# A kurtosis kernel: the batch finish as a bracket summed on TensorE, and the last group squared in one stretch

## The chip, the cores and the metric

One core of one Trainium2 chip runs the kernel; the program uses no other. Its engines work side by side: TensorE (matrix products, into a memory called PSUM), VectorE and ScalarE (element by element), and SyncE, which starts the transfers (DMA, loads and stores). The metric is device time in microseconds (us) of the whole program, as the median of several runs. A run is fast or slow by the rule that a slow one is over 1.5% above the fastest of the same kernel; only fast runs enter a ratio. The profiler records every execution; the trace shown for a kernel is one of them.

## The reference

For each of 1024 rows of 8192 values: subtract the mean, divide by the standard deviation, take the mean of the fourth power, subtract 3.

```python
mean = np.mean(x, axis=-1, keepdims=True)
std = np.std(x, axis=-1, keepdims=True)
z = (x - mean) / (std + 1e-8)
return (np.mean(z ** 4, axis=-1) - 3).astype(np.float32)
```

With the centred sums s2 = Σ(x-mean)² and s4 = Σ(x-mean)⁴ over n values this is n·s4/s2² - 3.

## The kernel before

The rows come in 18 groups, numbered 0 to 17. Most hold 64 rows, each row spread over k = 2 partitions of 4096 columns: 2 MB per group. For groups 6 to 16, TensorE transposes the 32 blocks of 128 columns into one PSUM tile and so adds them up (`tps`); VectorE adds the partitions of a row (`red`); a matmul with a column of -1/n gives the negated mean (`mps`); ScalarE copies it (`nmu`) and squares the tile in place with it as bias, with the sum in `s2`. The fourth powers, squares of the squares, are split: ScalarE takes the first columns, VectorE the rest. In groups 0 to 5 VectorE adds up the columns instead; in group 17 both engines share that, and the large square is cut into two halves.

The parts that matter here (comments added):

```python
    for i in range(L):
        warm_up(WARM.get(i, 0))
        mean(i)                                # PE: tps x32, mps; DVE: red; ACT: nmu
        square(i)                              # ACT, the large square
        if i >= 1:
            fourth_dve(i - 1, GROUPS[i - 1][2])
            load_next(i - 1)                   # a buffer is free: next load
        for f in steps.get(i, ()):             # one step of a batch's finish
            next(f, None)
        fourth_act(i, 0, GROUPS[i][2])
```

Results are finished in four batches of groups. The first three are finished in three steps spread over later groups, 7-8-9, 9-10-11 and 13-14-15:

```python
    def finish(b):
        fac = factor(b)             # PE: p2 = row sums of s2, times -1/n; DVE: fac = -1/p2^2
        yield
        w4 = scaled(b, fac, len(b)) # DVE: (qa + qd) * fac
        yield
        result(b, [w4])             # PE: pk = w4 summed per row; DVE: kr = pk - 3; store
```

In the traces each engine runs its instructions in the order in which these calls issue them.

## Time and profile before

| | before |
|---|---|
| median of 4 runs | 97.75 us (97.65 to 97.93) |
| span of the execution whose trace is shown | 97.1 us (a run of 98.84 us) |
| busy: ScalarE, VectorE, TensorE | 82%, 79%, 63% |
| start of the last large square S(17), of the last product kr | 87.87, 94.88 us |

S(i) is the start of group i's large square; for group 17 before, that of its first half. The span is shorter than the time: in the other runs of this kernel the time is 1.7 us above the span. Note that the traced execution was 1.1 us slower than the median.

### The profile page before, as it was taken

What the parts mean: (1) busy time and instruction counts of PE and PEld (TensorE: products, weight loads), DVE (VectorE), ACT (ScalarE), POOL (GpSimd) and SP (SyncE); (2) the same over time, 40 slices, a digit from 0 to 9 for tenths busy, and PEclk for the clock granted to TensorE, in tenths of its full rate; (3) what the DMA queues carried; (4) which work ended last, traced back from release to release, by engine and by line L of the source; (5) the groups of instructions that cost most, each with busy time, mean ns of one, the idle gap of its engine ahead of it and who ended that gap; (6) DMA issues with size and microseconds to landing.
All of it is one profiled execution on the core that took longest, in us unless ns stands there. A gap on an engine that the chain in (4) does not pass through costs nothing.

```text
span 97.1 us, 1280 instructions
## 1 busy us (share of the span) xinstructions
PE 60.7 (63%) x446; PEld 53.3 (55%) x446; DVE 76.5 (79%) x86; ACT 79.6 (82%) x89; POOL 4.7 (5%) x19
## 2 busy tenths in 40 slices
PE   0040201119998979729979797978979697951330
PEld 0040201015287869629969697877969596941310
DVE  1336819899995936989089899898999998999980
ACT  6055360899999999999549999999999999999960
POOL 6830000000000000000000000000000000000000
PEclk9999999999999999996699999999999999997555
DMA  2989999999999999999999999999999999300000
GB/s 57 390 302 405 425 432 432 432 432 426 404 422 406 435 423 429 412 428 409 433 421 428 412 417 403 410 424 404 419 418 413 414 411 397 123 1 0 0 0 4
DMA packets 5226, 33.63 MB, mean 346 GB/s; under 512 B 612, under 2 KB 612, under 8 KB 3812
## 3 DMA queue, kind: packets, MB, share of 16 engines
q1 hardware_dynamic: 5220, 33.56, 84.1%
q8 instruction: 3, 0.05, 0.2%
q14 instruction: 3, 0.02, 0.1%
HBM read 33.55 MB, written 0.00 MB: 346 GB/s over the span
## 4 chain that ended last, share of the span: by engine, by line
ACT 34%; DMA 28%; DVE 17%; PE 12%; issue 7%; ACTq 0%; DVEq 0%; SPq 0%
ACT xt L176 29%; DMA xt<-in_x_dram 28%; DVE xt L188 10%; PE tps L132 9%; DVE junk L149 6%; ACT xt L183 4%; PE pk L226 1%; DVE red L138 1%; ACT nmu L170 1%; PE mps L168 1%; PE mps L159 1%; PE p L204 0%; ACT wa L290 0%; DVE qd L188 0%; DVE kr L228 0%
## 5 line engine op out<-in xcount | busy, mean ns | idle before, releaser
L188 DVE CUSTOM_DVE_ANT_0 xt<-xt 128x3456 f32<-128x3456 f32 (+7 forms) x19 | 58.9, 3103 | 3.2 <-ACT xt L176 1.8
L176 ACT ACTIVATE xt<-xt,nmu 128x4096 f32<-128x4096 f32 (+2 forms) x19 | 60.4, 3177 | 0.6
L132 PE MATMUL tps<-ident,xt 128*128 128x128 f32 x380 | 45.8, 280 | 1.4 <-DMA xt<-in_x_dram 1.4
L132 PEld LDWEIGHTS tps<-ident,xt 128*128 128x128 f32 x380 | 43.6, 146 | 2.0 <-issue 1.4
L149 DVE CUSTOM_DVE_ANT_0 junk<-xt 128x2048 bf16<-128x2048 f32 (+3 forms) x7 | 10.2, 1453 | 6.9 <-DMA xt<-in_x_dram 6.9
L159 PE MATMUL mps<-part,blk 128*128 128x1 f32 x12 | 3.2, 332 | 19.3 <-DVE part L149 19.3
L159 PEld LDWEIGHTS mps<-part,blk 128*128 128x128 f32 x12 | 3.0, 304 | 20.7 <-issue 9.6
L183 ACT ACTIVATE xt<-xt 128x640 f32<-128x640 f32 (+5 forms) x15 | 12.9, 859 | 0.5
L170 ACT COPY nmu<-mps 128x1 f32<-128x1 f32 x18 | 2.6, 147 | 12.5 <-PE mps L159 10.0
L138 DVE TENSOR_REDUCE red<-tps 128x128 f32<-128x256 f32 x12 | 5.1, 424 | 6.8 <-PE tps L132 6.8
L168 PEld LDWEIGHTS mps<-negcol,red 128*128 128x128 f32 x22 | 3.3, 188 | 9.6 <-ACT xt L176 5.2
L168 PE MATMUL mps<-negcol,red 128*128 128x1 f32 x22 | 3.9, 247 | 7.3 <-DVE red L138 5.1
L256 PE MATMUL warm<-zeros 128*128 128x512 f32 x6 | 5.5, 1084 | 0.0
L176 ACT ACTIVATION_READ_ACCUMULATOR xt<-xt,nmu 128x1 f32 x19 | 3.5, 186 | 0.0
L256 PEld LDWEIGHTS warm<-zeros 128*128 128x128 f32 x6 | 1.9, 336 | 2.1 <-issue 2.1
L183 ACT ACTIVATION_READ_ACCUMULATOR xt<-xt 128x1 f32 x15 | 2.8, 187 | 0.0
L201 PE MATMUL p<-s,blk 128*128 128x1 f32 x2 | 0.6, 363 | 2.1 <-ACT xt L176 2.1
L70 ACT ACT_TABLE_LOAD x1 | 1.3, 1283 | 0.8 <-PEq L310 0.8
L201 PEld LDWEIGHTS p<-s,blk 128*128 128x128 f32 x2 | 0.5, 313 | 2.2 <-ACT xt L176 2.2
L83 POOL TENSOR_SCALAR_AFFINE_SELECT blk<-blk 128x128 f32<-128x128 f32 x3 | 1.7, 564 | 0.2
L80 POOL TENSOR_SCALAR_AFFINE_SELECT blk<-blk 128x128 f32<-128x128 f32 x3 | 1.7, 555 | 0.2
L188 DVE DVE_READ_ACCUMULATOR2_ANT qd<- 128x1 f32 x19 | 1.6, 82 | 0.0
(34 smaller groups left out, 14.1 us busy)
## 6 DMA issues: line engine op xcount, KB each, us to landing
xt<-in_x_dram SPq DMA_DIRECT2D x7, 1152.0 KB, 12.1
xt<-in_x_dram SPq DMA_DIRECT2D x9, 768.0 KB, 10.4
xt<-in_x_dram SPq DMA_DIRECT2D x7, 896.0 KB, 13.9
xt<-in_x_dram SPq DMA_DIRECT2D x3, 2048.0 KB, 11.9
xt<-in_x_dram SPq DMA_DIRECT2D x6, 512.0 KB, 10.8
xt<-in_x_dram SPq DMA_DIRECT2D x1, 1024.0 KB, 7.5
xt<-in_x_dram SPq DMA_DIRECT2D x1, 640.0 KB, 11.3
xt<-in_x_dram SPq DMA_DIRECT2D x1, 384.0 KB, 10.6
```

The costliest lines, as they stand in the source:

```text
L80: nc.gpsimd.affine_select(out=v, in_=v, pattern=[[-k, r], [0, k]], base=0, channel_multiplier=1, compare_op=AO.is_ge, fill=0.0)
L83: nc.gpsimd.affine_select(out=v, in_=v, pattern=[[k, r], [0, k]], base=k - 1, channel_multiplier=-1, compare_op=AO.is_ge, fill=0.0)
L132: nc.tensor.matmul(tps, lhsT=xts[i][:, c:c + P], rhs=ident, start=c == 0, stop=c == w - P, is_transpose=True)
L138: nc.vector.tensor_reduce(out=red.rearrange("p (r k) -> p r k", k=2), in_=tps.rearrange("p (r k) -> p r k", k=2).unsqueeze(2).to_broadcast ...
L149: nc.vector.tensor_tensor_reduce(out=junk[:, :h], in0=t[:, :h], in1=t[:, h:], scale=1.0, scalar=0.0, op0=AO.add, op1=AO.add, accum_out=part)
L159: nc.tensor.matmul(mps, lhsT=blk[k], rhs=added_halves(i, 0), start=True, stop=True)
L168: nc.tensor.matmul(mps, lhsT=pair_sums(tps), rhs=negcol, start=True, stop=True)
L170: nc.scalar.copy(nmu, mps)
L176: nc.scalar.activation(out=t, in_=t, func=AF.Square, bias=nmus[i], accum_out=s2[:, j + extra:j + extra + 1])
L183: nc.scalar.activation(out=t, in_=t, func=AF.Square, accum_out=qa[:, j:j + 1])
L188: nc.vector.tensor_tensor_reduce(out=t, in0=t, in1=t, scale=1.0, scalar=0.0, op0=AO.mult, op1=AO.add, accum_out=qd[:, j + extra:j + extra ...
L256: nc.tensor.matmul(warm, lhsT=zeros[:, :P], rhs=zeros, start=True, stop=True)
```

## The change

Its intent: less work on VectorE at the end, and a better balance. With fac = -1/p2² and p2 = -s2/n, the result is a product of two things that can each be summed over the row's partitions by TensorE: a bracket, (q0 + q1 + a multiple of p2²), and a factor row. So `-3` moves into the bracket as a matmul of `sq` = p2² with a scaled selector `sel3`, and the q tiles go into matmuls directly, without VectorE's add and multiply. The last group is squared in one stretch, all its columns transposed by TensorE, and its fourth powers follow in one part on ScalarE and two on VectorE. The splits of the fourth powers shift to VectorE.

```diff
-    (2, [2304, 1792], 640, 'PE'),               # x7, groups 6 to 12
-    (2, [1536, 1536, 1024], 512, 'PE'),         # x4, groups 13 to 16
-    (2, [1536, 1280, 768, 512], 1664, 'both'),
+    (2, [2304, 1792], 448, 'PE'),               # x8, groups 6 to 13
+    (2, [1536, 1536, 1024], 384, 'PE'),         # x2; then one with 256
+    (2, [1536, 1280, 768, 512], 1856, 'PE'),
...
     def finish(b):
         ... p2, rec, fac as in factor(b) ...
         yield
-        w4 = scaled(b, fac, len(b))
+        sq = fin.tile([P, n], f32, name="sq")
+        nc.scalar.activation(out=sq, in_=p2, func=AF.Square)
+        ...
+        nc.tensor.matmul(pf, lhsT=fac, rhs=sel, start=True, stop=True)
+        nc.tensor.matmul(pk, lhsT=sq, rhs=sel3[k], start=True, stop=False)
+        frow = fin.tile([n, r], f32, name="frow")
+        nc.scalar.activation(out=frow, in_=pf, func=AF.Copy, scale=-float(n_cols) / k)
         yield
-        result(b, [w4])
+        for q in quads:
+            nc.tensor.matmul(pk, lhsT=q, rhs=sel, start=False, stop=q is quads[-1])
+        kr = fin.tile([n, r], f32, name="kr")
+        nc.vector.tensor_mul(kr, pk, frow)
...
     mean(L)
-    square(L, h, 2 * h)
+    square(L)
     fourth_dve(L - 1, GROUPS[L - 1][2])
-    square(L, 0, h, extra=1)
-    fourth_dve(L, h, 2 * h)
     fourth_act(L, 0, a)
-    ... fac, w4, wa, the rest of the fourth powers, result ...
+    fourth_dve(L, LAST_CUT)
+    next(f)
+    fourth_dve(L, a, LAST_CUT, second=1)
+    next(f)
+    next(f, None)
```

More of the change, by code (lines that the diff above doesn't have):

```diff
@@ L22 @@
     (2, [4096], 1536, 'DVE'),
-    (2, [2304, 1792], 640, 'PE'),
-    (2, [2304, 1792], 640, 'PE'),
-    (2, [2304, 1792], 640, 'PE'),
-    (2, [2304, 1792], 640, 'PE'),
-    (2, [2304, 1792], 640, 'PE'),
-    (2, [2304, 1792], 640, 'PE'),
-    (2, [2304, 1792], 640, 'PE'),
-    (2, [1536, 1536, 1024], 512, 'PE'),
-    (2, [1536, 1536, 1024], 512, 'PE'),
-    (2, [1536, 1536, 1024], 512, 'PE'),
-    (2, [1536, 1536, 1024], 512, 'PE'),
-    (2, [1536, 1280, 768, 512], 1664, 'both'),
+    (2, [2304, 1792], 448, 'PE'),
+    (2, [2304, 1792], 448, 'PE'),
+    (2, [2304, 1792], 448, 'PE'),
+    (2, [2304, 1792], 448, 'PE'),
+    (2, [2304, 1792], 448, 'PE'),
+    (2, [2304, 1792], 448, 'PE'),
+    (2, [2304, 1792], 448, 'PE'),
+    (2, [2304, 1792], 448, 'PE'),
+    (2, [1536, 1536, 1024], 384, 'PE'),
+    (2, [1536, 1536, 1024], 384, 'PE'),
+    (2, [1536, 1536, 1024], 256, 'PE'),
+    (2, [1536, 1280, 768, 512], 1856, 'PE'),
 ]
@@ L38 @@
 SLOT_W = 4096
+LAST_CUT = 2688
 SLOT_OF = [0, 1, 2, 3, 0, 1, 2, 3, 4, 0, 1, 2, 3, 4, 0, 1, 2, 3]
-HALVES = 2
 @with_exitstack
@@ L97 @@
     block_matrix(2)
+    sel3 = {}
+    for k, b in blk.items():
+        sel3[k] = const.tile([P, P // k], f32, name=f"sel3_{k}")
+        nc.gpsimd.tensor_scalar_mul(
+            sel3[k], b.rearrange("p (r k) -> p r k", k=k)[:, :, 0], -3.0 * n_cols / k)
     junk = const.tile([P, 2048], bf16, name="junk")
     where = {}
-    stats = []
+    stats = {}
     for b in BATCHES:
-        n = len(b) + (b[-1] == L)
-        s2, qa, qd = (const.tile([P, n], f32, name=f"{t}_{b[0]}") for t in ("s2", "qa", "qd"))
+        n = len(b)
+        last = b[-1] == L
+        s2 = const.tile([P, n], f32, name=f"s2_{b[0]}")
+        quads = [const.tile([P, n], f32, name=f"q{t}_{b[0]}") for t in range(2 + last)]
         if any(GROUPS[i][2] == 0 for i in b):
-            nc.gpsimd.memset(qa, 0.0)
-        stats.append((s2, qa, qd))
+            nc.gpsimd.memset(quads[0], 0.0)
+        if last:
+            nc.gpsimd.memset(quads[2], 0.0)
+        stats[b[0]] = (s2, quads)
         for j, i in enumerate(b):
-            where[i] = (j, s2, qa, qd)
+            where[i] = (j, s2, quads)
     slots = [xpool.tile([P, SLOT_W], f32, name=f"xt{s}") for s in sorted(set(SLOT_OF))]
@@ L171, in mean, with square, fourth_dve @@
         nmus[i] = nmu
-    def square(i, c0=0, c1=None, extra=0):
-        j, s2, qa, qd = where[i]
-        t = xts[i][:, c0:c1]
-        nc.scalar.activation(out=t, in_=t, func=AF.Square, bias=nmus[i],
-                             accum_out=s2[:, j + extra:j + extra + 1])
+    def square(i):
+        j, s2, _ = where[i]
+        nc.scalar.activation(out=xts[i], in_=xts[i], func=AF.Square, bias=nmus[i],
+                             accum_out=s2[:, j:j + 1])
     def fourth_act(i, c0, c1):
-        j, s2, qa, qd = where[i]
+        j, _, quads = where[i]
         if c1 > c0:
             t = xts[i][:, c0:c1]
-            nc.scalar.activation(out=t, in_=t, func=AF.Square, accum_out=qa[:, j:j + 1])
-    def fourth_dve(i, c0, c1=None, extra=0):
-        j, s2, qa, qd = where[i]
+            nc.scalar.activation(out=t, in_=t, func=AF.Square, accum_out=quads[0][:, j:j + 1])
+    def fourth_dve(i, c0, c1=None, second=0):
+        j, _, quads = where[i]
         t = xts[i][:, c0:c1]
@@ L189, in fourth_dve, with finish @@
             out=t, in0=t, in1=t, scale=1.0, scalar=0.0,
-            op0=AO.mult, op1=AO.add, accum_out=qd[:, j + extra:j + extra + 1])
-    def factor(b):
-        s2 = stats[BATCHES.index(b)][0]
+            op0=AO.mult, op1=AO.add, accum_out=quads[1 + second][:, j:j + 1])
+    def finish(b):
+        s2, quads = stats[b[0]]
         n = len(b)
         k = KS[b[0]]
+        r = P // k
+        sel = blk[k].rearrange("p (r k) -> p r k", k=k)[:, :, 0]
         p2 = psfin.tile([P, n], f32, name="p2")
-        if b[-1] == L:
-            nc.tensor.matmul(p2[:, :n - 1], lhsT=blk[k], rhs=s2[:, :n - 1], start=True, stop=True)
-            nc.tensor.matmul(p2[:, n - 1:n], lhsT=blk[k], rhs=s2[:, n - 1:n], start=True, stop=False)
-            nc.tensor.matmul(p2[:, n - 1:n], lhsT=blk[k], rhs=s2[:, n:n + 1], start=False, stop=True)
-        else:
-            nc.tensor.matmul(p2, lhsT=blk[k], rhs=s2, start=True, stop=True)
+        nc.tensor.matmul(p2, lhsT=blk[k], rhs=s2, start=True, stop=True)
         rec = fin.tile([P, n], f32, name="rec")
@@ L209, in factor @@
             out=fac, in0=rec, scalar=-1.0, in1=rec, op0=AO.mult, op1=AO.mult)
-        return fac
-    def scaled(b, fac, n):
-        s2, qa, qd = stats[BATCHES.index(b)]
-        w4 = fin.tile([P, len(b)], f32, name="w4")
-        nc.vector.tensor_add(w4[:, :n], qa[:, :n], qd[:, :n])
-        nc.vector.tensor_mul(w4[:, :n], w4[:, :n], fac[:, :n])
-        return w4
-    def result(b, terms):
-        n = len(b)
-        k = KS[b[0]]
-        r = P // k
-        sel = blk[k].rearrange("p (r k) -> p r k", k=k)[:, :, 0]
-        pk = psfin.tile([n, r], f32, name="pk")
-        for j, t in enumerate(terms):
-            nc.tensor.matmul(pk, lhsT=t, rhs=sel, start=j == 0, stop=j == len(terms) - 1)
+        yield
+        sq = fin.tile([P, n], f32, name="sq")
+        nc.scalar.activation(out=sq, in_=p2, func=AF.Square)
+        pf = psfin.tile([n, r], f32, name="pf")
+        pk = psfin.tile([n, r], f32, name="pk")
+        nc.tensor.matmul(pf, lhsT=fac, rhs=sel, start=True, stop=True)
+        nc.tensor.matmul(pk, lhsT=sq, rhs=sel3[k], start=True, stop=False)
+        frow = fin.tile([n, r], f32, name="frow")
+        nc.scalar.activation(out=frow, in_=pf, func=AF.Copy, scale=-float(n_cols) / k)
+        yield
+        for q in quads:
+            nc.tensor.matmul(pk, lhsT=q, rhs=sel, start=False, stop=q is quads[-1])
         kr = fin.tile([n, r], f32, name="kr")
-        nc.vector.tensor_scalar_add(kr, pk, -3.0)
+        nc.vector.tensor_mul(kr, pk, frow)
         dst = out[ROWS[b[0]]:ROWS[b[-1] + 1]].rearrange("(g r) -> g r", r=r)
         nc.sync.dma_start(out=dst, in_=kr)
-    def finish(b):
-        fac = factor(b)
-        yield
-        w4 = scaled(b, fac, len(b))
-        yield
-        result(b, [w4])
     held = {}
@@ L272 @@
         fourth_act(i, 0, GROUPS[i][2])
-    k, _, a, _ = GROUPS[L]
-    h = n_cols // k // 2
-    b = BATCHES[-1]
-    n = len(b)
-    s2, qa, qd = stats[-1]
+    a = GROUPS[L][2]
+    f = finish(BATCHES[-1])
     mean(L)
-    square(L, h, 2 * h)
+    square(L)
     fourth_dve(L - 1, GROUPS[L - 1][2])
-    square(L, 0, h, extra=1)
-    fourth_dve(L, h, 2 * h)
     fourth_act(L, 0, a)
-    fac = factor(b)
-    w4 = scaled(b, fac, n - 1)
-    wa = fin.tile([P, n], f32, name="wa")
-    nc.gpsimd.memset(wa, 0.0)
-    nc.scalar.activation(out=wa[:, n - 1:], in_=qa[:, n - 1:n], func=AF.Copy, scale=fac[:, n - 1:])
-    fourth_dve(L, a, h, extra=1)
-    nc.vector.scalar_tensor_tensor(
-        out=w4[:, n - 1:], in0=qd[:, n:], scalar=qd[:, n - 1:n], in1=fac[:, n - 1:],
-        op0=AO.add, op1=AO.mult)
-    result(b, [wa, w4])
+    fourth_dve(L, LAST_CUT)
[3 more added lines that the diff above has]
+    next(f, None)
 _INS = ['x']
```

## The prediction

> **What bounds the kernel now.** I read the chain of work that ended last first: it says which engine the time passes through.
>
> ```profile
> ACT 34%; DMA 28%; DVE 17%; PE 12%; issue 7%; ACTq 0%; DVEq 0%; SPq 0%
> ...
> 43.44 5.37 PE tps L132 x32
> ...
> 59.73 3.81 ACT xt L176 x2
> 63.54 0.02 issue
> 63.56 0.55 ACT xt L183
> ```
>
> In order of time it is loads up to 43.3 us, then TensorE for two groups (its 32 transposes give a group's column sums), and from 54.95 us ScalarE almost without a gap. I number the groups 0 to 17 as in the list at the head of the kernel and call S(i) the start of the large square L176 of group i. From the timeline S(8) to S(17) are 42.83, 49.98, 54.95, 59.73, 64.47, 69.22, 73.86, 78.50, 83.14, 87.87: a step of 4.64 to 4.75.
>
> Then the timeline of one such step, to see what lies beside the square (group 14; the transposes are those of group 15):
>
> ```profile
> 73.06 3.89 DVE L188 CUSTOM_DVE_ANT_0 xt<-xt 128x3584 f32<-128x3584 f32 x1 [0.26 <-ACT xt L176]
> 73.86 3.73 ACT L176 ACTIVATE xt<-xt,nmu 128x4096 f32<-128x4096 f32 x1
> 75.75 1.04 PE L132 MATMUL tps<-ident,xt 128*128 128x128 f32 x8
> ...
> 77.16 0.42 DVE L138 TENSOR_REDUCE red<-tps 128x128 f32<-128x256 f32 x1
> ...
> 77.73 0.35 PE L168 MATMUL mps<-negcol,red 128*128 128x1 f32 x2 [0.93 <-ACT xt L176]
> ...
> 78.22 3.71 PE L132 MATMUL tps<-ident,xt 128*128 128x128 f32 x32
> 78.24 0.19 ACT L183 ACTIVATION_READ_ACCUMULATOR xt<-xt 128x1 f32 x1
> 78.33 0.14 ACT L170 COPY nmu<-mps 128x1 f32<-128x1 f32 x1
> 78.50 3.72 ACT L176 ACTIVATE xt<-xt,nmu 128x4096 f32<-128x4096 f32 x1
> ```
>
> The reader is to see that transposes of group 15 (L132, ended at 76.8) run under the square of group 14 (73.86 to 77.7). Only so is the mean of 15 (reduce L138, matmul L168, copy L170) ready when ScalarE finishes its fourth powers. That overlap, not the busy share, sets the step.
>
> Third, the groups by shape, for durations, and the granted clock:
>
> ```profile
> L183 ACT ACTIVATE xt<-xt 128x640 f32<-128x640 f32 x7 | 5.2, 738 | 0.2
> ...
> L183 ACT ACTIVATE xt<-xt 128x512 f32<-128x512 f32 x4 | 2.5, 632 | 0.1
> ```
>
> ```profile
> 44.00:45.00 1.00, 1.00 (x9) 1.00 (x8) 1.00 (x1) 1.00 (x1) 0.00 (x0) 0.73 1.04 436
> 45.00:46.00 1.00, 1.00 (x7) 1.00 (x6) 0.93 (x4) 1.00 (x1) 0.00 (x0) 0.50 1.02 426
> 46.00:47.00 1.00, 1.00 (x7) 1.00 (x6) 0.00 (x0) 0.97 (x3) 0.00 (x0) 0.50 0.98 408
> 47.00:48.00 1.00, 1.00 (x7) 1.00 (x6) 0.00 (x0) 0.50 (x2) 0.00 (x0) 0.56 1.05 434
> ```
>
> The third number from the right is the granted clock. After TensorE had idled 1.4 us (42.06 to 43.44, waiting for the load of group 9) its clock fell to one half from about 44.46 to 47.88, and the 32 transposes took 5.35 us instead of 3.69: about 1.7 us lost.
>
> **What the Trainium skill says.** "TensorE: Matmul & The Clock Gate", section "Part 3: Packing small matmuls — row/col tiling", says matmuls are "strict FIFO, no reordering"; only weight loads may be pulled ahead. The trace before agrees as far as it goes: transposes of group i+1 always start after the mean matmul L168 of group i. The same page, "Part 1: The HAM clock gate (the "warmup" mystery)", says that the clock halves after an idle window of about 3.4 us and is restored after a busy one, the windows running free. The trace agrees: 44.46 to 47.88 is 3.42 us, and the last drop, at 88.9 us by the windows, is 13 such windows after the first. "ScalarE: Activation LUTs", section "What happens when an `exp` ACTIVATE runs", gives 0.833 ns per element; the rows above give 106 ns per 128 elements, or 0.83.
>
> **The change part by part.**
> (a) Balance. ScalarE's fourth powers shrink from 640 to 448 elements (groups 6 to 12), 512 to 448 (13), 384 (14, 15) and 256 (16). At 0.83 ns that saves 0.16 us per group for 6 to 12, then 0.05, 0.11, 0.11 and 0.21. In the ScalarE-bound stretch 10 to 16 this is 0.96 us. VectorE's part grows by as many elements; its rows of 3456 (3.76 us) and 2048 (2.29 us) give 1.04 ns each, so 192 elements cost 0.20 us; its step is then about 3.89 + 0.34 for the reduce = 4.25 us, still under ScalarE's 3.84 + 0.58 + 0.17 = 4.59 us.
> (b) Last group. All 32 tiles are transposed, no VectorE sum. One square of 3.84 us (to the next instruction) replaces two halves; fourth powers of 1408 follow it, 1.55 us; reciprocal and factor 0.30; then 832 more, 1.0 us; its accumulator, the last two-pass matmul and the wait to the product 0.5. The product kr starts 3.84 + 1.55 + 0.30 + 1.0 + 0.5 = 7.2 us after S(17). Before it was 94.88 - 87.87 = 7.0. This part gains nothing, because VectorE can begin only when the whole square has ended: +0.2 us.
> (c) Batch finish. VectorE loses an add and a multiply per batch (0.16 us each). ScalarE gains a small square sq and a copy frow; TensorE gains pf, and pk in three or four parts. This moves one dependence. The built program's order on TensorE at the second step of each batch (in group 8, 10 and 14) is: mean matmul of group i, pf, pk from sq (which waits for ScalarE), then the transposes of group i+1. On ScalarE, sq stands behind the large square of group i. So the transposes, which ran under that square, cannot start before it has ended. Before, the second step had no matmul, and VectorE's w4 was long ready when pk came.
>
> The cost of such a stall, with a clock at full: sq starts 3.86 us after S(i); with itself, the signal and the pk matmul the transposes start at S(i) + 4.35 (my estimate: 0.2 for sq from the 0.15 of copy L170, the rest from the spacing of small matmuls at 49.7 to 50.1). Transposes 3.69; from their end to the next square 1.17 (at 53.77 to 54.95 before: reduce, matmul, copy). S(i+1) = S(i) + 9.2 against 4.6.
>
> Going through the groups:
> - S(8) is 42.55 (ScalarE's step of 4.59 twice from 33.35, less a little held back by VectorE). Stall 1: transposes of group 9 start at 46.9 instead of 43.44; with full clock S(9) = 51.75, +1.8 against 49.98. Small, because a load wait and a slow stretch are swallowed.
> - S(10): TensorE now follows itself (mean matmul, three small matmuls, 3.69, 1.17): 5.2 against 4.97: +0.25.
> - Stall 2: 9.2 against 4.78: +4.4. S(12): 5.15 against 4.74: +0.4. S(13), S(14): 4.65 each, -0.1.
> - Stall 3: 9.25 against 4.64: +4.6. S(16): 4.85, +0.2. S(17): 4.6 against 4.73, -0.1.
> - Tail +0.2.
> Sum 11.65 us.
> - Clock. In each stall TensorE idles 4 to 5 us, longer than the 3.4 us window, so it will be at half clock when the transposes start. At half clock 3.42 us passed some 14 tiles instead of 31, a loss of 0.54 us per us. Depending on where the window's edge falls, the transposes run cold for 1.7 to 5 us, a loss of 0.9 to 2.6; I take 1.65. Three times: 5.0 us.
> Total 16.7 us on 97.7: 114.4, stated as 114.0 us.
>
> The loads follow late too: group 15's may start only when VectorE is done with group 10, at about 72.6 instead of 62.5 us, and DMA then rests some 4 to 6 us. But group 15 lands near 80 us, ahead of its transposes at 88: I count nothing for it.
>
> **The rivals.**
> 1. What the author wanted: no stall, ScalarE 0.96 us shorter, tail 0.2 longer: 97.0 us. For it: the steady steps are ScalarE's. Against: the order of matmuls; it would need transposes to overtake a waiting matmul.
> 2. The stall is there but at full clock: 109.4 us. For it: the clock record is coarse. Against: only 1.4 us of idle brought half clock before.
> 3. VectorE becomes the bound by taking more elements: 4.25 against 4.59 per step says no; in groups 15 and 16 (3.96 and 4.09 + 0.34) it comes close. It would give about 97.5 without the stall.
> 4. Late loads add to the stalls: if groups 15 to 17 landed 4 us later than worked out, up to 118.
>
> **Range and chances.** The lower end is rival 2 with one or two cold stretches, 111; the upper end takes the worst window edges in two stalls or some load wait, 117. That the program's order holds on the chip I give 95 in 100: slower 0.95, same 0.03, faster 0.02.
>
> **What would show it right or wrong.** Right: transposes of groups 9, 11 and 15 starting only after the preceding square and a short square sq, ScalarE idle about 4.6 us or more before the copy nmu of 11 and 15, three stretches of clock 0.5, chain of waits with far more TensorE, and steps of about 4.6 us between the stalls. Wrong: those transposes already running under the square (rival 1), or clock 1.0 in them (rival 2). A tail from S(17) to kr far from 7.2 us would make part (b) wrong.

## More of the kernel before

From the page of the kernel before, the row of loads over 40 equal slices of the span, in GB/s:

```profile
GB/s 57 390 302 405 425 432 432 432 432 426 404 422 406 435 423 429 412 428 409 433 421 428 412 417 403 410 424 404 419 418 413 414 411 397 123 1 0 0 0 4
```

The loads run at 397 to 435 GB/s from the fourth slice to the 34th, and end in the 35th.

## The result, and the profile after

| | before | changed |
|---|---|---|
| median | 97.75 us (97.65 to 97.93, 4 runs) | 114.97 us (114.33 to 115.77, 4 runs) |
| span of the trace shown | 97.1 us | 113.2 us |
| busy ScalarE, VectorE, TensorE | 82%, 79%, 63% | 69%, 68%, 58% |
| S(17); kr; end of span | 87.87; 94.88; 97.1 | 102.96; 110.22; 113.2 |

The ratio is 1.1763, with a 95% interval of 1.1686 to 1.184. Ratios here are the mean time of one kernel's fast runs over that of the other's fast runs of the same rounds, so not quite the ratio of the medians.

First the chain of waits of the changed kernel: shares by engine, and one stretch of it in order of time (start, length, what).

```profile
ACT 47%; PE 29%; DMA 10%; DVE 6%; issue 3%; SPq 1%; DVEq 0%
...
83.00 3.80 ACT xt L184 x2
86.80 0.07 ACT sq L217
86.87 0.04 issue
86.92 0.34 PE pk L221 x2
87.26 5.21 PE tps L141 x32
```

TensorE's share went from 12% to 29%, though it does hardly more work. The reader sees one stall in five lines: the large square of group 14, then `sq`, then the matmul that reads it, and only then the 32 transposes of group 15.

The timeline of the same stretch shows who sat idle (idle time and what ended it in brackets):

```profile
83.00 3.71 ACT L184 ACTIVATE xt<-xt,nmu 128x4096 f32<-128x4096 f32 x1
...
86.70 0.16 ACT L217 ACTIVATE sq<-p 128x10 f32<-128x10 f32 x1
...
86.92 0.34 PE L221 MATMUL pk<-sel,sq 128*10 128x64 f32 x2 [3.93 <-ACT sq L217]
...
87.19 5.26 PE L141 MATMUL tps<-ident,xt 128*128 128x128 f32 x32
...
92.49 0.42 DVE L147 TENSOR_REDUCE red<-tps 128x128 f32<-128x256 f32 x1 [6.28 <-PE tps L141]
...
93.39 0.16 ACT L179 COPY nmu<-mps 128x1 f32<-128x1 f32 x1 [5.92 <-PE mps L177]
93.58 3.72 ACT L184 ACTIVATE xt<-xt,nmu 128x4096 f32<-128x4096 f32 x1
```

Before, the transposes of group 15 lay under the square of group 14. Now TensorE idles 3.93 us beside that square, and then VectorE and ScalarE idle about 6 us each beside TensorE. The step from S(14) to S(15) is 10.58 us instead of 4.64.

The waits summed up, first of the changed kernel, then the two corresponding lines of before (engine, tile, line, what it waited for: us in total, times, longest):

```profile
DVE red L147 <- PE tps L141: 23.3, 8, 6.9
ACT nmu L179 <- PE mps L177: 18.9, 6, 6.5
```

```profile
DVE red L138 <- PE tps L132: 6.8, 8, 2.9
...
ACT nmu L170 <- PE mps L168: 2.3, 1, 2.3
```

ScalarE waited 18.9 us for means of transposed groups, against 2.3 before. The difference, 16.6 us, is close to the whole loss.

Last the granted clock of TensorE and the loads, in 40 slices, for the changed kernel:

```profile
PEclk9999999999999999679995579999998599998555
...
GB/s 96 371 408 446 417 434 434 413 420 373 381 432 429 433 407 430 425 412 430 420 346 402 349 342 203 17 326 365 364 346 426 366 23 0 1 0 0 0 0 3
```

There are three dips of the clock besides the one at the end, one at each stall, and one hole in the loads, at 68 to 74 us: the second stall held back VectorE, so buffers came free late. The transposes of group 15, which use the data that came late, waited 0 us for them.

Eleven starts of large squares say it in numbers, S(7) to S(17): 37.57, 42.29, 52.74, 57.72, 68.93, 73.81, 78.39, 83.00, 93.58, 98.45, 102.96. Three steps are of 10.45, 11.21 and 10.58 us, the others of 4.5 to 5.0.

### The profile page after: what moved, and what is told of

Same layout as the page of the kernel before. It is cut to its first block, busy times and chain, and to the rows that moved or that the text cites. A ratio compares the mean times of both kernels' runs of the same rounds, so it can differ in the third digit from the quotient of the medians.

```text
span 113.2 us, 1311 instructions
## 1 busy us (share of the span) xinstructions
PE 66.2 (58%) x468; PEld 57.8 (51%) x468; DVE 76.6 (68%) x75; ACT 78.5 (69%) x94; POOL 5.9 (5%) x22
## 4 chain that ended last, share of the span: by engine, by line
ACT 47%; PE 29%; DMA 10%; DVE 6%; issue 3%; SPq 1%; DVEq 0%
ACT xt L184 40%; PE tps L141 24%; DMA xt<-in_x_dram 10%; ACT xt L191 5%; DVE red L147 2%; PE mps L177 2%; DVE junk L158 2%; DVE xt L196 1%; PE pk L226 1%; ACT nmu L179 1%; SPq L135 1%; PE pk L221 1%; PE mps L168 1%; PE pf L220 0%; PE p L209 0%
## 5 line engine op out<-in xcount | busy, mean ns | idle before, releaser
L196 DVE CUSTOM_DVE_ANT_0 xt<-xt 128x3648 f32<-128x3648 f32 (+9 forms) x19 | 60.7, 3196 | 2.0 <-ACT nmu L179 1.1
L141 PE MATMUL tps<-ident,xt 128*128 128x128 f32 x384 | 50.1, 294 | 0.5 <-DMA xt<-in_x_dram 0.5
L141 PEld LDWEIGHTS tps<-ident,xt 128*128 128x128 f32 x384 | 47.3, 154 | 1.7 <-DMA xt<-in_x_dram 1.1
L179 ACT COPY nmu<-mps 128x1 f32<-128x1 f32 x18 | 2.7, 152 | 28.7 <-PE mps L177 18.9
L158 DVE CUSTOM_DVE_ANT_0 junk<-xt 128x2048 bf16<-128x2048 f32 (+2 forms) x6 | 9.7, 1617 | 6.8 <-DMA xt<-in_x_dram 6.8
L191 ACT ACTIVATE xt<-xt 128x448 f32<-128x448 f32 (+6 forms) x15 | 11.4, 760 | 0.4
L221 PE MATMUL pk<-sel,sq 128*2 128x16 f32 (+3 forms) x8 | 1.2, 246 | 11.9 <-ACT sq L217 7.9
L249 PE MATMUL warm<-zeros 128*128 128x512 f32 x6 | 4.6, 936 | 0.0
L209 PE MATMUL p<-s,blk 128*128 128x2 f32 (+3 forms) x8 | 1.7, 284 | 4.1 <-ACT xt L184 4.1
L226 PE MATMUL pk<-blk,q 128*5 128x64 f32 (+3 forms) x18 | 2.0, 245 | 0.0
L220 PE MATMUL pf<-blk,fac 128*2 128x16 f32 (+3 forms) x8 | 1.2, 233 | 1.4 <-DVE fac L213 1.4
```

The source lines that it names most:

```text
L141: nc.tensor.matmul(tps, lhsT=xts[i][:, c:c + P], rhs=ident, start=c == 0, stop=c == w - P, is_transpose=True)
L158: nc.vector.tensor_tensor_reduce(out=junk[:, :h], in0=t[:, :h], in1=t[:, h:], scale=1.0, scalar=0.0, op0=AO.add, op1=AO.add, accum_out=part)
L179: nc.scalar.copy(nmu, mps)
L191: nc.scalar.activation(out=t, in_=t, func=AF.Square, accum_out=quads[0][:, j:j + 1])
L196: nc.vector.tensor_tensor_reduce(out=t, in0=t, in1=t, scale=1.0, scalar=0.0, op0=AO.mult, op1=AO.add, accum_out=quads[1 + second][:, j:j + 1])
L209: nc.tensor.matmul(p2, lhsT=blk[k], rhs=s2, start=True, stop=True)
```

## The experiments

The record has the result of every kernel as correct. They ran in three sets of 4, 4 and 3, each with runs of the kernel before beside it (medians 98.28, 98.03 and 97.96 us; the sets share some of these runs). The changed kernel itself ran beside a kernel before of 97.75 us, so between sets the ratios compare better than the times.

**The stall itself.** r1_bracket_late moves one line: `pk` from `sq` goes into the third step, where the other matmuls of the bracket are.

```diff
-        nc.tensor.matmul(pk, lhsT=sq, rhs=sel3[k], start=True, stop=False)
         frow = ...
         yield
+        nc.tensor.matmul(pk, lhsT=sq, rhs=sel3[k], start=True, stop=False)
         for q in quads:
```

> The changed kernel with one matmul moved: pk from sq is issued in the third step of each batch, after the mean matmul of the next group, beside the matmuls from the q tiles; everything else, sq and frow on ScalarE and the count of matmuls, stays. Theory (the matmul waiting for sq holds back the next group's transposes): all three stalls go, S(i) steps are about 4.6 us, no transposes start after the square they used to lie under, time 97.0 us (96.6 to 97.6). Rival (the extra ScalarE and TensorE instructions of the new finish, or VectorE's larger share, cost the time): stays above 105 us.

Measured: 99.61 us, ratio 1.0163 (1.0107 to 1.0219). All three stalls are gone; the timeline round group 14 reads:

```profile
71.86 1.53 PE L141 MATMUL tps<-ident,xt 128*128 128x128 f32 x12
71.94 3.72 ACT L184 ACTIVATE xt<-xt,nmu 128x4096 f32<-128x4096 f32 x1
...
74.42 2.40 PE L141 MATMUL tps<-ident,xt 128*128 128x128 f32 x20 [1.03 <-DMA xt<-in_x_dram]
...
75.66 0.15 ACT L217 ACTIVATE sq<-p 128x10 f32<-128x10 f32 x1
```

The transposes are back under the square, and `sq` is where it was. One moved matmul gives back 15.4 us by the medians (114.97 - 99.61; by the ratios 15.7) of the 17.2 us lost, so the rival (the extra instructions or VectorE's larger share cost the time) falls for these 15.4. But I had expected 97.0 us, and the steps are not 4.6 us throughout; the one from S(14) to S(15) is 6.07. The third line says why: TensorE waits for a load. I come back to this with p1 to p4.

r4_sq_early leaves every matmul in its place and makes the source ready instead: `sq` is issued one step earlier.

```diff
+        if b[-1] != L:
+            sq = ... ; nc.scalar.activation(out=sq, in_=p2, func=AF.Square)
         yield
-        sq = ... ; nc.scalar.activation(out=sq, in_=p2, func=AF.Square)
+        if b[-1] == L:
+            sq = ... ; nc.scalar.activation(out=sq, in_=p2, func=AF.Square)
```

> The changed kernel with all matmuls in their places; only the square sq is issued one step earlier on ScalarE (behind the large square of group 7, 9 and 13), so that it is ready when pk from sq comes. Theory: the place of the matmul is harmless when its source is ready; no stall, about 97.0 us (96.6 to 97.8), same as r1_bracket_late. Rival (small matmuls between mean and transposes cost time by being there): stays near 115 us.

Measured: 99.72 us, ratio 1.0142 (1.0063 to 1.0221), the same as r1 within the intervals, and like r1 it misses its 97.0 us, by 2.7 us. In group 14 `pk` from `sq` no longer waits, and the transposes of group 15 start with the square:

```profile
72.49 0.27 PE L225 MATMUL pk<-sel,sq 128*10 128x64 f32 x2
...
72.67 3.74 ACT L184 ACTIVATE xt<-xt,nmu 128x4096 f32<-128x4096 f32 x1
...
72.70 3.71 PE L141 MATMUL tps<-ident,xt 128*128 128x128 f32 x32
```

A small matmul between a mean and the next transposes is harmless; a small matmul that waits there is not. Two different repairs of the same wait give the same time: that settles the wait as the cause.

r2_one_stall is r1 with the old place kept for the third batch only (`if b[0] == 3` ahead of the early line, `!= 3` ahead of the late one).

> As r1_bracket_late, but the third batch (finished in groups 13 to 15) keeps pk from sq in its second step: one stall left of three, that in group 14. Theory (stalls add up, each costs its wait and a cold run of transposes, with nothing in the loads behind it): 97.0 + 4.6 + 0.1 + 0.9 to 2.6 for the clock = 102.6 to 104.3 us, centre 103.3. Rival (the late loads after stalls 1 and 2 are what costs at the end): under 101 us.

Measured: 105.68 us; fast runs 104.41 and 105.33, ratio 1.07 (1.0612 to 1.0788). This is above my expectation, because that was built on 97.0 for the kernel without stalls. Against r1 it is 0.07 - 0.016 = 0.054 of 98 us, 5.3 us for one stall, uncertain by about 1 us (two fast runs); I had added 5.6 to 7.3. The rival (under 101 us, the cost comes from late loads behind the first two stalls) falls.

**The clock.** r3_warm_fill keeps the stalls and fills TensorE's wait with dummy work.

```diff
+        if b[-1] != L:
+            warm_up(4)
         nc.tensor.matmul(pk, lhsT=sq, rhs=sel3[k], start=True, stop=False)
```

> The changed kernel with its three stalls, and four dummy matmuls of 512 columns (0.91 us each at full clock) ahead of each pk from sq, so that TensorE works during most of the 4 us for which it waits. Theory (of 17.2 us, about 5.3 are transposes at half clock): transposes of groups 9, 11 and 15 take 3.7 us each, the clock record stays at 1.0 there, time 109.3 to 110.3 us. Rival (the transposes are slow after the wait for another reason than the clock, or dummy work delays them as much): 114 to 116 us.

Measured: 109.27 us, ratio 1.1134 (1.1064 to 1.1205), at the lower edge of what I expected. The page's clock row and, from the timeline, the third stall:

```profile
PEclk9999999999999999999999999999999999999755
```

```profile
81.60 1.02 PE L251 MATMUL warm<-zeros 128*128 128x512 f32 x2
...
82.96 0.28 PE L223 MATMUL pk<-sel,sq 128*10 128x64 f32 x2 [0.34 <-ACT sq L217]
...
83.17 3.71 PE L141 MATMUL tps<-ident,xt 128*128 128x128 f32 x32
```

The clock stays full and the transposes take 3.71 us in place of 5.26. Useless work of 3.7 us per stall makes the kernel 5.7 us faster by the medians, 6.2 us by the ratios (1.1763 - 1.1134 of 98 us, uncertain by about 1 us). So of the loss, about 6 us is the half clock after the wait, and the rest the wait. This is also the case that the prediction priced as its second rival, stalls at full clock: 109.4 us. The three steps with a stall here, from one large square to the next, are 8.98, 8.91 and 8.97 us.

**Why r1 is not 97 us.** p1_split_only is the kernel before with nothing but the new splits of the fourth powers.

```diff
-    (2, [2304, 1792], 640, 'PE'),               # groups 6 to 12
+    (2, [2304, 1792], 448, 'PE'),
-    (2, [1536, 1536, 1024], 512, 'PE'),         # groups 13 to 16
+    (2, [1536, 1536, 1024], 448, 'PE'),         # then 384, 384, 256
```

> The kernel before with only the numbers of its fourth powers changed to those of the change (448 for groups 6 to 13, 384, 384, 256 for 14 to 16); loads, last group and finish untouched. My term of the prediction (ScalarE sets the steps): 0.96 us faster, ratio 0.990. Rival, from r1_bracket_late, whose transposes of groups 12, 14 and 15 waited for loads: the loads arrive one group per 4.9 us, the steps cannot be shorter on the whole, so nothing is gained: ratio 0.998 to 1.005.

Measured: 99.03 us, ratio 1.0083 (0.9997 to 1.0168): no gain, and above the rival's range too; the interval doesn't exclude a small loss. p2_bracket_only is the kernel before with the bracket finish, wait removed as in r1, for the first three batches only.

> The kernel before with only the finish of the first three batches changed to the bracket form, with pk from sq in the third step so that nothing stalls; splits, last group and last finish untouched. Theory (the bracket itself is free once its wait is gone): ratio 0.998 to 1.004. Rival (the bracket form costs by its extra matmuls and ScalarE instructions what r1_bracket_late lacks): ratio 1.01 or more.

Measured: 98.22 us, ratio 1.0017 (0.9955 to 1.008). The bracket is free where nothing waits on it.

The traces say what sets the pace; no run made the loads themselves shorter. "Perfetto Trace Analysis", section "Roofline", of the Trainium skill puts the limit of one core's 16 DMA engines at about 435 GB/s; the rows stand at 400 to 435 in nearly every slice. A group of 2.1 MB then takes about 4.9 to 5.0 us at 417 to 425 GB/s, longer than ScalarE's step of 4.59 to 4.75. From 30 to 80 us all 16 DMA engines of the kernel before were busy (share 1.01, 417 GB/s), so buffers that come free late do not set this pace. From the DMA records of the traces, first and last load packet, kr, and the end:

| kernel | first load starts | last load lands | kr starts, after last load | end of span, after kr |
|---|---|---|---|---|
| before | 1.82 | 85.12 | 9.76 | 2.25 |
| p1_split_only | 1.83 | 85.35 | 9.79 | 2.25 |
| p2_bracket_only | 1.82 | 84.08 | 9.49 | 2.25 |
| r1_bracket_late | 1.82 | 85.29 | 9.72 | 2.94 |
| r4_sq_early | 1.82 | 84.72 | 9.74 | 2.80 |
| p3_one_load_fewer (below) | 1.84 | 83.96 | 9.55 | 2.83 |
| p4_late_one_load_more (below) | 1.83 | 84.50 | 9.80 | 2.27 |
| changed kernel | 1.87 | 91.36 | 18.86 | 2.93 |

Without a stall, kr follows the last load by 9.5 to 9.8 us whatever the splits and whatever the form of the finish. Apart from the changed kernel, how long the loads take differs by up to 1.4 us, and most of that is there in the first 10 us, long before the kernels differ in their splits: the loads then run at a mean of 298 GB/s in before, 297 in p1, 333 in p2 and 338 in p3, which differs from before in group 13 alone. The 0.4 MB between them is about 1 us of loading at 417 GB/s. So where the last load of a single trace lands says little about its kernel. The stretch in which ScalarE seemed to set the time was one in which it caught up with the loads, and the 0.96 us saved there is spent waiting: in p1's trace ScalarE waits 3.3 us for means of transposed groups, in seven places, against 2.3 us in one place before.

**The end of the span.** The last column shows a difference that I had not thought of: 2.25 to 2.27 us in the kernels with 40 transfers (36 loads, 4 stores), 2.8 to 2.9 us in those with 39; the changed kernel loads group 13 in two pieces instead of three. Two kernels test this from both sides.

```diff
 p3_one_load_fewer (before):  group 13  [1536, 1536, 1024] -> [2304, 1792]
 p4_late_one_load_more (r1):  group 13  [2304, 1792] -> [1536, 1536, 1024]
```

> The kernel before with the load of group 13 in two pieces instead of three, as in the changed kernel; nothing else. In the trace of the changed kernel and of r1 to r4 the span ends 2.7 to 3.0 us after the last product kr, before 2.2. If the count of SyncE's instructions or the place of the last store's semaphore in the closing waits makes that: the end goes from 2.2 to 2.8 us or so, ratio 1.004 to 1.008. If not: the end stays at 2.2 us, ratio 0.998 to 1.003.

> r1_bracket_late with the load of group 13 in three pieces again, so that SyncE has as many transfers as before. If the count makes the longer end: from kr to the end of the span 2.2 us, about 0.6 us faster than r1_bracket_late (ratio to before about 1.010). If not: 2.8 us and a ratio near 1.016.

Measured: p3 ends 2.83 us after kr, p4 2.27 us: the count of transfers moves the end by 0.6 us in both directions. The times say the same less sharply: 98.11 us, ratio 1.0051 (0.9967 to 1.0134), and 98.97 us, ratio 1.0115 (1.0024 to 1.0206). The drains among SyncE's closing instructions, first p3 and then p4 (count, shortest, median and longest duration in ns, first and last start):

```profile
L321 SPq DRAIN  x3: 7/7/125, 95.5 to 95.9; - x3
```

```profile
L304 SPq DRAIN  x3: 7/7/7, 95.8 to 96.1; - x3
```

In both kernels the last store lands 1.2 us after it is issued. With 39 transfers one of the closing drains takes 125 ns and starts about 0.4 us after the instruction ahead of it, for which the trace shows no reason. The traces of r2 and r3 (39 transfers, 2.81 us) and of v1 to v3 below (40 transfers, 2.09 to 2.27 us) fit. What SyncE does there stays open. That it changes with 39 against 40 transfers is shown; but the last store's semaphore is then also the last but one that SyncE waits for, instead of the last, and no run tells the count from this place.

**A version that beats both?** v1_halves_bracket takes the loads, splits (but for 1600 instead of 1664 columns in group 17) and two half squares of before, and the bracket without its wait in all four batches.

```diff
 (against r1_bracket_late)
-    square(L)
+    square(L, h, 2 * h)
     fourth_dve(L - 1, GROUPS[L - 1][2])
-    fourth_dve(L, LAST_CUT)
+    square(L, 0, h, extra=1)
+    fourth_dve(L, h, 2 * h)
```

> The bracket finish in all four batches with its wait gone, but the splits, loads and last group of before (two half squares, VectorE's sum of 256 columns). Theory (loads set the pace, only what follows the last load counts; the bracket takes w4's add and multiply off VectorE's last stretch and the halves let it begin early): kr about 0.4 us sooner after the last load than before, ratio 0.994 to 0.999. Rival (the last finish is slower by its three more matmul pairs at half clock): ratio 1.001 to 1.006.

Measured: 98.4 us, ratio 1.004 (0.9982 to 1.0098). In its trace kr follows the last load by 9.46 us, 0.3 sooner than before, but the time does not show it: the ratio lies in the rival's range, with an interval too wide to decide. v2_small_last cuts the last 64 rows into two groups of 32, since only work after the last load counts, and issues the second one's mean ahead of the preceding fourth powers; these two groups make a fifth batch, and the splits are others again; v3 gives more of group 16's fourth powers to ScalarE.

```diff
-    (2, [1536, 1280, 768, 512], 1856, 'PE'),
+    (4, [1024, 1024], 384, 'PE'),
+    (4, [1024, 512, 512], 1152, 'PE'),
...
         square(i)
+        if i == L - 1:
+            mean(L)
         if i >= 1:
             fourth_dve(i - 1, GROUPS[i - 1][2])
```

> The bracket finish without the wait, and the last group of 64 rows cut into two groups of 32 rows (2048 columns each), both squared before the last fourth powers, as many transfers as before. Theory (with loads setting the pace, the work after the last load counts, and half a group is half the work): kr 1.0 to 2.0 us sooner after the last load, ratio 0.98 to 0.992. Rival (the small groups bring their fixed cost twice, means and small instructions, and VectorE is behind anyway): ratio 0.995 or more.

> As v2_small_last with 1152 instead of 768 columns of group 16's fourth powers on ScalarE. If VectorE is the engine that ends last in v2, 384 columns fewer there are 0.40 us: faster than v2 by up to 0.4 us; if ScalarE ends last, slower by 0.3 us.

Measured: 102.61 us, ratio 1.0364 (1.0269 to 1.0458), and 102.0 us, ratio 1.0414 (1.0362 to 1.0466): both slower, and v3 tells nothing against v2. The timeline of v2 shows that I had built the fault of the change again, on another engine:

```profile
86.43 3.59 PE L142 MATMUL tps<-ident,xt 128*128 128x128 f32 x16
...
90.06 0.69 DVE L148 TENSOR_REDUCE red<-tps 128x128 f32<-128x512 f32 x1 [4.00 <-PE tps L142]
90.66 3.61 DVE L197 CUSTOM_DVE_ANT_0 xt<-xt 128x3328 f32<-128x3328 f32 x1
```

The reduce of the last group, put ahead of 3.6 us of fourth powers, waits 4.0 us for transposes that themselves came late and at half clock (16 tiles in 3.59 us), while VectorE's ready work stands behind it. The wait is about as long as the loss (102.61 against 97.96 us; by the fast runs 3.6 us), but no run takes it away again, so that it makes the whole loss is not shown. No version beat the kernel before beyond the noise.

## Why the prediction was right

It gave 114.0 us, 111 to 117; 114.97 was measured. Point by point, by its own steps:

- *The moved dependence, step (c).* Right, and shown by r1 and r4: removing the wait from either side removes all three long steps.
- *The size of a stall at full clock.* Predicted: the transposes start 4.35 us after S(i), the step is 9.2 us. Measured: 4.21, 4.11 and 4.19 us in the changed kernel, and steps of 8.91 to 8.98 in r3. So 0.2 us too much per stall, most of it because `sq` starts 3.71 us after S(i) and not 3.86.
- *The clock.* Predicted 1.65 us three times, 5.0 in all. The transposes took 5.12, 5.98 and 5.26 us; against 3.69 that is 1.43 + 2.29 + 1.57 = 5.3 us, and r3 won back 5.7 to 6.2. The rate of 0.54 us lost per us at half clock was wrong: the first of the three lay 2.95 us in the half-clock stretch and lost 1.43, which is 0.49, and the prediction's own lines give (5.35 - 3.69)/3.42 = 0.49. It hardly entered, since 1.65 us was taken.
- *Between the stalls.* Predicted steps of 5.2, 5.15, 4.65, 4.65, 4.85 and 4.6; measured 4.98, 4.88, 4.58, 4.61, 4.87 and 4.51.
- *The late loads.* I counted nothing for them: right. Group 15's load came about when predicted (VectorE was done with group 10 at 72.1 us, predicted 72.6), the loads rested, and the transposes of group 15 did not wait.
- *The tail, step (b).* Predicted 7.2 us from S(17) to kr, measured 7.26.
- *What the sum lacked.* The closing after kr, 0.7 us longer. And I added my difference to the median while reading positions from a traced run that was 1.1 us slower than the median. On the traces kr came 15.3 us later, where I had 16.7; on the medians the kernel is 17.2 us slower. The stalls that I made a little too long and what was missing at the end cancelled; that the total came within 1 us of the measured time is in part luck.
- *Step (a) and the first rival's price.* Wrong, though it hardly entered the number. I took the ScalarE-bound look of the chain for a bound and priced a kernel without stalls at 97.0 us. r1 measured 99.61, and p1 shows that the new splits gain nothing, because the loads set the pace. In the changed kernel the loads ran ahead during the stalls, so there the steps of 4.6 us were right. The reading of the chain also left out VectorE, 17% of it, before 30 us and from 87 us on.
- *A source.* The 0.833 ns per element stands in "ScalarE: Activation LUTs" one heading further down than the prediction says, under "Step-by-step: what each stage is for".

What stays open: with p4, the closing corrected, the changed kernel without stalls is still about 1% slower than before (1.0024 to 1.0206), while its trace shows kr as soon after the last load. The first suspect is the new splits: p1, which has nothing else, and p4 both have spans 0.6 us longer than before (means of the fast runs), v1, with the old splits and the bracket in all batches, 0.1 us. That fits a small loss by the splits in place of the gain of 0.96 us, but it is no larger than the scatter of the loads, so it is not shown. And in the runs of r1 the time exceeds the span by 1.8 to 2.8 us, before by 1.7. I have no explanation for that.

## What to carry to other kernels

Before a small instruction is put into an engine's queue, ask when its source will be ready and what stands behind it: on an in-order engine the wait of a 0.3 us matmul is paid by all that follows, and by every engine that this feeds. Look at when the work is issued, not only at what it costs; the same matmul one step later, or its source one step earlier, took away all three stalls. And an engine that is busy without a gap is not yet the bound: compare its step with the time that the loads take for one step's data.

## What the Trainium skill lacked or had wrong

- "TensorE: Matmul & The Clock Gate", "Part 4: PE-mode transpose", says that the full clock does not engage for transposes since they don't count as busy in the same way. Here 32 transposes took 3.69 us, 115 ns each, at a granted clock of 1.0; in the kernel before the clock came back to 1.0 at 47.88 us, with nothing but transposes on TensorE since 43.44; in r1_bracket_late the clock stayed at full speed until 89.7 us, with transposes as nearly all of TensorE's work after 28 us.
- The same page, "Part 1: The HAM clock gate (the "warmup" mystery)", speaks of an idle window. The window need not be wholly idle: in the kernel before, the clock fell at 44.46 us though TensorE had been busy about 1.4 of the preceding 3.4 us (a mean matmul of 0.35 us and 1.02 us of transposes). In the changed kernel the half-clock stretches last 3.41, 6.83 and 3.41 us, whole windows, as the page says.
- No page that I found says that small activations can hide behind a large one that sums: in the changed kernel the fourth powers of groups 8, 10 and 14 start 3.83, 3.83 and 3.87 us after the large square, with `sq` and `frow` in between, and those of group 7, without them, 3.84 us after it.
- No page that I found has the longer end of a program with one transfer fewer: 2.83 against 2.25 us from kr (p3_one_load_fewer against before), 2.27 against 2.94 (p4_late_one_load_more against r1_bracket_late).
